# Both scan directions in one process: their small products alternate between the two column halves of the matrix array

## The chip, the cores and the metric

The kernel runs on one core of one Trainium2 chip. The metric is the device time of one execution in microseconds (us), lower is better. The core's engines work in parallel, each through its own instruction queue in order: TensorE (PE, matrix products, with its weight loads shown apart as PEld), VectorE (DVE), ScalarE (ACT), GpSimd (POOL), and SyncE (SP), which starts transfers. A product takes its operands from the 128 partitions of the on-chip memory and writes into the 128 partitions of the accumulator memory, which has banks of 512 columns.

## The reference

One encoder layer is applied to two request groups, a prompt of 512 tokens and a sample of 1024 tokens, of width 1024. It has a SwiGLU block, a mixer and a second SwiGLU block, each with normalisation, shift, scale and gate. Half of the mixer's channels go through windowed averages, the other half (8 heads of 64 channels) through a recurrence that runs over the tokens once forwards and once backwards:

```python
def step(S, inp):
    r_t, w_t, k_t, v_t, na_t, b_t = inp
    sa = jnp.einsum('bhvk,bhk->bhv', S, na_t)
    S = S * w_t[:, :, None, :] + sa[..., None] * b_t[:, :, None, :] + v_t[..., None] * k_t[:, :, None, :]
    y = jnp.einsum('bhvk,bhk->bhv', S, r_t)
    return S, y
...
ys.append(wkv_scan(r, decay, k_d, v, kk, a, reverse=(d == 1)))
...
y = ys[0] + ys[1]
```

## The kernel before

**Dense work.** Tokens are handled in three blocks of 512 (two of the sample, one of the prompt). The SwiGLU blocks, the mixer's input and its output projection are products of 128x128 weights with 128x512 activations. Each is done as three products of a split number: `whi`, `wlo` are the upper and lower parts of the weights, `hh`, `hl` (and `gh`, `gl`) those of the activations; `u`, `v` and `y` are the banks in which the results stand. One generator (`mainA`, then `mainB` and `mainC`) issues all dense work in a fixed sequence, and where it needs something that isn't there yet, it stops.

**The scan.** The recurrence is done in chunks of `L` = 64 tokens, for two heads at a time (one head on partitions 0 to 63, the other on 64 to 127). There are 8 pairs of heads and group, and they make 12 "macros" of 8 chunks: 96 chunks in each of the two directions `d`. `scan_prep` makes the operands of a macro half (4 chunks), `scan_inv` inverts its triangular matrices, `scan_state` carries the 64x64 states `SBD` through the chunks, and `scan_post` normalises the output. `MU` holds three operand arrays: `MA` and `MR` (64x64 matrices of a chunk) and `UV`. For every chunk and direction `scan_state` has three stages:

- W: the product of `AR` with the state (`sb<-SBD,AR` in the profile: 128 rows of the array, 64 columns, 128 moving elements; left out in the first chunk of a pair) and two 64x64 products of `MA` with `UV` (`sb<-MU`, 64*64), all into `Wp`; ScalarE copies `Wp` to `iw` (`XN<-sb`) and writes the state times the chunk's decay to `s0p`;
- U: two 64x64 products with `iw` (`sb<-XN,MU`) into `Up`; ScalarE copies them to `UV` (`MU<-sb`);
- the state's increment (`sb<-MU,BKt`, 128 rows) and the output (`sb<-AR,SBD`, 64 rows, and `sb<-MU` with 128 rows), where the two heads' products write to partitions 0 to 63 and 64 to 127 in turn; VectorE then makes the new state from the increment and `s0p`.

Each direction has a bank of its own (`sb` with the number 9080 for the forward one, 9081 for the backward one). In it `Wp` and `Up` stand on partitions 0 to 63 in both directions. A product of 32-bit numbers is two records in the trace, each with a weight load.

**What sets the order.** The program is planned while it is built. Every generator is a process; a `yield WAIT` gives back control, and `run_until` starts the process of the smallest `prio` number whose last result should be there by a table of estimated durations (`Estimate`). The two directions were two processes, `scan_state(sb, 0)` and `scan_state(sb, 1)`, both of `prio` 0, and the dense generator (`prio` 3) fills what is left, one product at a time. Each engine then executes its instructions in that order. While the scan is going on (`scanning`), the lower halves `wlo` of the weights are made by VectorE, otherwise by GpSimd or VectorE. All engine instructions carry line 161 in the profile, since one helper issues them; they are told apart by their tiles.

Of the kernel before, what the change touches and what calls it, by code (L numbers as in the profile page):

```python
# [12 lines left out]
AF = mybir.ActivationFunctionType  # L13
ALU = mybir.AluOpType
# [3 lines left out]
P = 128  # L18
# [5 lines left out]
L = 64  # L24
# [14 lines left out]
GO, WAIT, CHAIN, PIPE = -1.0, -2.0, -3.0, -4.0  # L39
# [133 lines left out]
def encoder_kernel(ctx, tc, x_prompt, x_sample, c_prompt, c_sample, ada_w, ada_b, n1_pre, n1_post,  # L173
# [5 lines left out]
    V, S, G, T, SY = (Queue(est, *q) for q in (("V", nc.vector), ("S", nc.scalar), ("G", nc.gpsimd), ("T", nc.tensor),  # L179
                                               ("Y", nc.sync)))  # L180
# [21 lines left out]
    def mt(shape, tag, bufs, dt=F32, pool=None):  # L202
        return est.ring((pool or mp).tile(shape, dt, name=nm(tag), tag=tag, bufs=bufs), (id(pool), tag), bufs)
# [10 lines left out]
    def spawn(gen, prio):  # L214
        procs.append(Proc(gen, prio))

    def run_until(stop):

        while not stop():
            clock = est.free["T"]
            for p_ in procs:
                if p_.cond is not None and p_.cond():
                    p_.cond = None
                    p_.ready = max(p_.ready, clock)
            live = [p_ for p_ in procs if p_.cond is None]
            assert live
            now = [p_ for p_ in live if p_.ready <= clock]
            if now:  # L230
                p_ = min(now, key=lambda q: q.prio)
            else:
                p_ = min(live, key=lambda q: q.ready)
                est.free["T"] = p_.ready
            est.last = 0.0
            try:
                r = next(p_.gen)
            except StopIteration:
                procs.remove(p_)
                continue  # L240
            if callable(r):
                p_.cond = r
            elif isinstance(r, tuple):
                p_.ready = r[0]
            elif r == GO:
                p_.ready = 0.0
            elif r == PIPE:
                p_.ready = est.last - PIPE_LEAD
            elif r == CHAIN:
                p_.ready = est.last - CHAIN_LEAD  # L250
            else:
# [700 lines left out]
    GT = (TB, 2 * TB)  # L952
# [192 lines left out]
    GL = 4 * L  # L1145

    def st_(sb, shape, tag, bufs=1):
        return mt(shape, tag, bufs, pool=sb.sp)
# [180 lines left out]
            flags.add(("inv", m, gi))  # L1329
            give("inv")  # L1330

    def scan_state(sb, d):
        AR, BKt, UV, MA, MR, SBD, PL, bank = sb.AR, sb.BKt, sb.UV, sb.MA, sb.MR, sb.SBD, sb.PL, sb.bank[d]
        Wp = bank[0:64, 0:P]
        Up = bank[0:64, P:2 * P]
        for m, (i_, hf) in enumerate(macros):
            g, p = pairs[i_]
            nblk = GT[g] // GL
            nh = nblk // 2
            for c8 in range(8):  # L1340
                gi, c = c8 // 4, c8 % 4
                if c == 0:
                    yield has(("inv", m, gi))
                zero = hf == 0 and c8 == 0
                lastc = hf == nh - 1 and c8 == 7
                us = [gi * 16 + d * 8 + h * 4 + c for h in range(2)]
# [12 lines left out]
                S.activation(UV[0:64, gi, d, c].rearrange("p h f -> p (h f)"), Up, AF.Copy)  # L1359
                yield WAIT  # L1360
                if not lastc:
                    for h in range(2):
                        hs_ = slice(64 * h, 64 * h + 64)
                        mm(bank[hs_, 0:L], BKt[:, gi, d, c, hs_], UV[:, gi, d, c, h, :])
                yo = 256 + c * L
                if not zero:
                    for h in range(2):
                        hs_ = slice(64 * h, 64 * h + 64)
                        mm(bank[hs_, yo:yo + L], SBD[hs_, d, hs_], AR[hs_, gi, d, c, 1, :], stop=False)
                for h in range(2):  # L1370
                    mm(bank[64 * h:64 * h + 64, yo:yo + L], UV[:, gi, d, c, h, :], MR[:, us[h], :], start=zero)
                if not lastc:
                    for h in range(2):
                        hs_ = slice(64 * h, 64 * h + 64)
                        pl_ = PL[hs_, m % 2, gi, d, c:c + 1]
                        if zero:
                            V.tensor_scalar(SBD[hs_, d, hs_], bank[hs_, 0:L], pl_, None, op0=ALU.mult)
                        else:
                            V.scalar_tensor_tensor(SBD[hs_, d, hs_], bank[hs_, 0:L], pl_, s0p[hs_, hs_],
                                                   ALU.mult, ALU.add)  # L1380
                if c == 3:
                    t = 2 * hf + gi
                    gb = t if d == 0 else nblk - 1 - t
                    if t == 0 and i_ not in sb.yT:
                        if i_ >= 1:
                            yield has(("post", i_ - 1))
                        if i_ not in sb.yT:
                            sb.yT[i_] = st_(sb, [P, GT[g]], "yT")
                    o = sb.yT[i_][:, gb * GL:(gb + 1) * GL]
                    if d == 1:  # L1390
                        o = rev(o)
                    if t >= nh:
                        V.tensor_tensor(o, o, bank[:, 256:512], ALU.add)
                    else:
                        S.activation(o, bank[:, 256:512], AF.Copy)
                    flags.add(("st", m, gi, d))
                yield WAIT

    def scan_post(sb):
# [181 lines left out]
    with tc.tile_pool(name="late", bufs=1, reuse_waits="tile") as lp:  # L1581
        sb = ScanBufs(lp)
        scanning.append(sb)

        spawn(scan_state(sb, 0), 0)
        spawn(scan_state(sb, 1), 0)
        spawn(scan_inv(sb, 0), PRIO_INV)
        spawn(scan_inv(sb, 1), PRIO_INV)
        spawn(scan_prep(sb), PRIO_PREP)
        spawn(scan_post(sb), PRIO_POST)  # L1590

        run_until(has(("m", 1), ("m", 0)))
        scanning.clear()
# [35 lines left out]
```

## Time and profile before

| | |
|---|---|
| median of 3 runs | 3785.25 us (3784.39 to 3792.8) |
| the profiled execution | 3780.28 us; its span from the first to the last instruction 3778.3 us |
| busy share of the span: PE, DVE, ACT, POOL | 95%, 53%, 38%, 37% |
| instructions of PE | 19579 products, as many weight loads |
| the scan | from 1270 us to 2698 us of the span |
| mean granted clock of PE | 0.956 |

Busy time counts an instruction from its start to its modelled end, and products are pipelined, so a busy PE can still be issued faster or slower: how many microseconds a group of products takes is read from the starts of its first product and of the next group's first. The granted clock is the share of PE's full clock over a stretch; a row of the timeline merges neighbours of one kind and gives their first start, and "xcount" is the number of records.

### The profile page before, as it was taken

Reading aid. Unit: us, or ns where it says so; the run is one execution under the profiler, and the core shown is the slowest. Engines: PE = TensorE matmul, PEld = TensorE weight load, DVE = VectorE, ACT = ScalarE, POOL = GpSimd, SP = SyncE. Lnnn points to the kernel's source line nnn. Section 1 sums busy time; section 2 is a strip of 40 time slices with the busy share of each in tenths; the row PEclk is TensorE's granted clock in tenths of the full one; section 3 lists DMA queues with packets and bytes.
Section 4 is the critical chain, followed back from the end, with each engine's and each line's share of the span. In section 5 each row is a group of like instructions: output and inputs, shape, how many; then the busy total and the mean of one; then the engine's idle time right before and its main releaser. Section 6 shows DMA issues by size and latency. Waiting matters only on the chain. (4 is left out here: it accounts for less than half of the span.)

```text
span 3778.3 us, 53665 instructions
## 1 busy us (share of the span) xinstructions
PE 3593.2 (95%) x19579; PEld 2703.6 (72%) x19579; DVE 1999.0 (53%) x3801; ACT 1424.1 (38%) x2776; POOL 1410.4 (37%) x1716
## 2 busy tenths in 40 slices
PE   7999999998999999999899989799999999999998
PEld 4667878876676767666666666567787778877886
DVE  3128362237237778776777776778448622242223
ACT  3324342225335434344345433343334432234222
POOL 2333444443132222234234233432344344444444
PEclk8999999998999999999889978599999999999999
DMA  7655343334344322222324343222254333334332
GB/s 274 235 181 169 91 154 92 99 90 134 123 128 126 93 67 88 82 71 87 117 76 122 96 137 105 74 73 77 87 159 151 103 115 98 93 109 132 94 95 78
DMA packets 557980, 432.11 MB, mean 114 GB/s; under 512 B 27029, under 2 KB 511572, under 8 KB 553620
## 3 DMA queue, kind: packets, MB, share of 16 engines
q1 hardware_dynamic: 524900, 379.90, 32.8%
q10 hardware_dynamic: 32816, 48.78, 4.1%
q8 instruction: 155, 2.54, 0.3%
q14 instruction: 109, 0.89, 0.1%
HBM read 367.23 MB, written 61.34 MB: 113 GB/s over the span
## 5 line engine op out<-in xcount | busy, mean ns | idle before, releaser
L161 POOL TENSOR_TENSOR wlo<-wraw,whi 128x512 fp32r<-128x512 f32 x672 | 892.6, 1346 | 1294.2 <-ACT whi L161 866.5
L161 DVE TENSOR_TENSOR y<-y,y 128x512 f32<-128x512 f32 x480 | 327.2, 684 | 848.9 <-PE y L161 847.9
L161 ACT ACTIVATE whi<-wraw 128x512 fp32r<-128x512 f32 x938 | 559.2, 622 | 181.6 <-PE v L161 139.7
L161 PE MATMUL u<-hh,whi 128*128 128x512 f32 x1392 | 568.2, 408 | 10.2 <-ACT zraw L161 4.0
L161 PE MATMUL u<-hl,whi 128*128 128x512 f32 x1392 | 564.3, 405 | 14.1 <-POOL hl L161 7.4
L161 PE MATMUL v<-hh,whi 128*128 128x512 f32 x1392 | 562.4, 404 | 12.8 <-ACT hh L161 7.6
L161 PE MATMUL u<-hh,wlo 128*128 128x512 f32 x1392 | 567.0, 407 | 0.1
L161 PE MATMUL v<-hl,whi 128*128 128x512 f32 x1392 | 561.0, 403 | 1.0 <-DVE hl L161 1.0
L161 PE MATMUL v<-hh,wlo 128*128 128x512 f32 x1392 | 560.7, 403 | 0.0
L161 PE MATMUL y<-gh,whi 128*128 128x512 f32 x1056 | 425.6, 403 | 12.8 <-DVE y L161 10.8
L161 PE MATMUL y<-gl,whi 128*128 128x512 f32 x1056 | 422.7, 400 | 0.2 <-DVE gl L161 0.2
L161 PE MATMUL y<-gh,wlo 128*128 128x512 f32 x1056 | 422.2, 400 | 0.0
L161 POOL TENSOR_TENSOR XN<-XN 64x126 f32<-64x126 f32 (+22 forms) x744 | 322.4, 433 | 93.6 <-DVE XN L161 18.5
L161 PEld LDWEIGHTS u<-hl,whi 128*128 128x128 f32 x1392 | 266.6, 191 | 81.5 <-DVE hl L161 12.6
L161 ACT ACTIVATE gh<-s 128x512 fp32r<-128x512 f32 x132 | 83.3, 631 | 639.3 <-DVE s L161 639.3
L161 PEld LDWEIGHTS u<-hh,whi 128*128 128x128 f32 x1392 | 266.3, 191 | 80.9 <-issue 7.7
L161 PEld LDWEIGHTS v<-hh,whi 128*128 128x128 f32 x1392 | 264.2, 190 | 82.9 <-ACT hh L161 11.3
L161 PEld LDWEIGHTS u<-hh,wlo 128*128 128x128 f32 x1392 | 266.3, 191 | 68.8 <-issue 9.5
L161 PEld LDWEIGHTS v<-hl,whi 128*128 128x128 f32 x1392 | 264.4, 190 | 66.3 <-issue 4.9
L161 PEld LDWEIGHTS v<-hh,wlo 128*128 128x128 f32 x1392 | 264.8, 190 | 62.9 <-issue 5.9
L161 DVE TENSOR_TENSOR wlo<-wraw,whi 128x512 fp32r<-128x512 f32 x266 | 206.4, 781 | 150.6 <-ACT whi L161 149.8
L161 PEld LDWEIGHTS y<-gh,whi 128*128 128x128 f32 x1056 | 199.9, 189 | 67.2 <-DVE y L161 12.0
(252 smaller groups left out, 4504.6 us busy)
## 6 DMA issues: line engine op xcount, KB each, us to landing
wraw<-in_f_w_dram SPq DMA_DIRECT2D x792, 256.0 KB
ada<-in_ada_w_dram SPq DMA_DIRECT2D x32, 1024.0 KB
wraw<-in_w_in_dram SPq DMA_DIRECT2D x98, 256.0 KB
xk<-xs ACTq DMA_DIRECT2D x96, 256.0 KB
xs<-y ACTq DMA_DIRECT2D x48, 256.0 KB
wraw<-in_w_out_dram SPq DMA_DIRECT2D x48, 256.0 KB
in_k<-zk SPq DMA_DIRECT2D x48, 128.0 KB
in_kk<-zkk SPq DMA_DIRECT2D x48, 128.0 KB
```

What stands on the lines that cost most here:

```text
L161: return f(*args, **kw)
```

## The change

There is now one process for both directions. W of both directions is issued together, then U of both, then the third stage of both. In W and U the products alternate between the directions, and the backward direction's `Wp` and `Up` stand on partitions 64 to 127 of its bank, so that neighbouring products use different halves of the array's columns. The four copies by ScalarE stand together in pairs, and the two `s0p` come behind the copies of `Up` and no longer behind the first copy of `Wp`. In the third stage the increments of both directions come first and then, per direction, the output products. Number, shape and operands of the scan's products are the same.

```diff
-    def scan_state(sb, d):
+    def scan_state(sb):
...
+        half = [slice(64 * h, 64 * h + 64) for h in both]
+        Wp = [sb.bank[d][half[d], 0:P] for d in both]
+        Up = [sb.bank[d][half[d], P:2 * P] for d in both]
...
                 if not zero:
-                    mm(Wp, AR[:, gi, d, c, 0, :], SBD[:, d, :], stop=False)
-                for h in range(2):
-                    mm(Wp[:, h * L:(h + 1) * L], MA[64:128, us[h], :], UV[64:128, gi, d, c, h, :], start=zero)
-                wsb = sb.iw[:, d * P:(d + 1) * P]
-                S.activation(wsb, Wp, AF.Copy)
+                    for d in both:
+                        mm(Wp[d], AR[:, gi, d, c, 0, :], SBD[:, d, :], stop=False)
+                for h in both:
+                    for d in both:
+                        mm(Wp[d][:, hl_(h)], MA[64:128, us(d, h), :], UV[64:128, gi, d, c, h, :], start=zero)
+                for d in both:
+                    S.activation(wsb[d], Wp[d], AF.Copy)
+                yield WAIT
+                for h in both:
+                    for d in both:
+                        mm(Up[d][:, hl_(h)], MA[0:64, us(d, h), :], wsb[d][:, hl_(h)])
+                for d in both:
+                    S.activation(UV[0:64, gi, d, c].rearrange("p h f -> p (h f)"), Up[d], AF.Copy)
                 if not zero and not lastc:
-                    s0p = st_(sb, [P, P], f"s0p{d}")
-                    S.activation(s0p, SBD[:, d, :], AF.Copy, scale=PL[:, m % 2, gi, d, c:c + 1])
-                yield WAIT
-                for h in range(2):
-                    mm(Up[:, h * L:(h + 1) * L], MA[0:64, us[h], :], wsb[:, h * L:(h + 1) * L])
-                S.activation(UV[0:64, gi, d, c].rearrange("p h f -> p (h f)"), Up, AF.Copy)
+                    for d in both:
+                        s0p[d] = st_(sb, [P, P], f"s0p{d}")
+                        S.activation(s0p[d], SBD[:, d, :], AF.Copy, scale=PL[:, m % 2, gi, d, c:c + 1])
                 yield WAIT
                 if not lastc:
-                    for h in range(2):
...
+                    for d in both:
+                        for h in both:
+                            mm(sb.bank[d][half[h], 0:L], BKt[:, gi, d, c, half[h]], UV[:, gi, d, c, h, :])
...
-        spawn(scan_state(sb, 0), 0)
-        spawn(scan_state(sb, 1), 0)
+        spawn(scan_state(sb), 0)
```

PE's queue before, at the second chunk of the scan: W of the forward direction (`sb_9080`), W of the backward one (`sb_9081`), three dense products, and the forward U.

```order
L161 MATMUL sb_9080<-SBD_9077,AR_9073 64x128
L161 MATMUL sb_9080<-MU_9075 64x64 x2
L161 MATMUL sb_9081<-SBD_9077,AR_9073 64x128
L161 MATMUL sb_9081<-MU_9075 64x64 x2
L161 MATMUL v_10093<-hh_8728,whi_9961 128x512
L161 MATMUL v_10093<-hl_8729,whi_9961 128x512
L161 MATMUL v_10093<-hh_8728,wlo_9962 128x512
L161 MATMUL sb_9080<-XN_9076,MU_9075 64x64 x2
```

The same W now:

```order
L161 MATMUL sb_9080<-SBD_9077,AR_9073 64x128
L161 MATMUL sb_9081<-SBD_9077,AR_9073 64x128
L161 MATMUL sb_9080<-MU_9075 64x64
L161 MATMUL sb_9081<-MU_9075 64x64
L161 MATMUL sb_9080<-MU_9075 64x64
L161 MATMUL sb_9081<-MU_9075 64x64
L161 MATMUL v_10081<-hh_8728,wlo_9962 128x512
```

The four groups of W have become two, each of them alternating between the directions.

PE's queue before, at U of the same chunk (the product in front of the first row is dense, and the next U is the next chunk's):

```order
L161 MATMUL sb_9080<-XN_9076,MU_9075 64x64 x2
L161 MATMUL v_10093<-hh_8728,whi_9961 128x512
L161 MATMUL v_10093<-hl_8729,whi_9961 128x512
L161 MATMUL sb_9081<-XN_9076,MU_9075 64x64 x2
L161 MATMUL v_10093<-hh_8728,wlo_9962 128x512
```

And now:

```order
L161 MATMUL v_10081<-hh_8728,wlo_9962 128x512
L161 MATMUL sb_9080<-XN_9076,MU_9075 64x64
L161 MATMUL sb_9081<-XN_9076,MU_9075 64x64
L161 MATMUL sb_9080<-XN_9076,MU_9075 64x64
L161 MATMUL sb_9081<-XN_9076,MU_9075 64x64
L161 MATMUL v_10081<-hh_8728,whi_9961 128x512
```

Dense products stood between the two directions' U, and now they stand in front of and behind both. In the whole program such a pair of U was divided in 78 of 96 chunks, and is now in none; the stretches of other work between two dense products of the scan's time are 379 and were 483.

ACT's queue before, in the next chunk (`s0p` is the decayed state, `XN<-sb` the copy of W, `MU<-sb` that of U):

```order
L161 ACTIVATE XN_9076<-sb_9080 64x128
L161 ACTIVATE s0p_10142<-SBD_9077,PL_9079 128x128
L161 ACTIVATE XN_9076<-sb_9081 64x128
L161 ACTIVATE s0p_10148<-SBD_9077,PL_9079 128x128
L161 ACTIVATE whi_10152<-wraw_9916 128x512
L161 ACTIVATE MU_9075<-sb_9080 64x128
L161 ACTIVATE MU_9075<-sb_9081 64x128
```

And now:

```order
L161 ACTIVATE XN_9076<-sb_9080 64x128
L161 ACTIVATE XN_9076<-sb_9081 64x128
L161 ACTIVATE MU_9075<-sb_9080 64x128
L161 ACTIVATE MU_9075<-sb_9081 64x128
L161 ACTIVATE s0p_10108<-SBD_9077,PL_9079 128x128
L161 ACTIVATE s0p_10110<-SBD_9077,PL_9079 128x128
L161 ACTIVATE whi_10124<-wraw_9916 128x512
```

The two `s0p` have moved from between the copies to behind them.

The plan of everything else moves with it, since the same planner sets it. At one place the dense generator has stopped (it waits for the block's normalisation after the prompt's first SwiGLU). PE's queue there before, with the directions at different stages and preparation products (`sM`) among them:

```order
L161 MATMUL sb_9080<-XN_9076,MU_9075 64x64 x2
L161 MATMUL sb_9081<-SBD_9077,AR_9073 64x128
L161 MATMUL sb_9081<-MU_9075 64x64 x2
L161 MATMUL sb_9080<-MU_9075,BKt_9074 64x64 x2
L161 MATMUL sb_9080<-AR_9073,SBD_9077 64x64 x2
L161 MATMUL sb_9080<-MU_9075 64x64 x2
L161 MATMUL sM_15818<-in_wa_15717,w2s_151 128x256
L161 MATMUL sM_15819<-in_wa_15717,w2s_151 128x256
L161 MATMUL sb_9081<-XN_9076,MU_9075 64x64 x2
```

And PE's queue there now, where U follows W, and the increment follows U, with nothing between:

```order
L161 MATMUL sb_9080<-MU_9075 64x64
L161 MATMUL sb_9081<-MU_9075 64x64
L161 MATMUL sb_9080<-XN_9076,MU_9075 64x64
L161 MATMUL sb_9081<-XN_9076,MU_9075 64x64
L161 MATMUL sb_9080<-XN_9076,MU_9075 64x64
L161 MATMUL sb_9081<-XN_9076,MU_9075 64x64
L161 MATMUL sb_9080<-MU_9075,BKt_9074 64x64 x2
L161 MATMUL sb_9081<-MU_9075,BKt_9074 64x64 x2
```

One direction's stage stood between the other's, and now both directions stand at the same stage. Over all, 7210 of the program's 11556 dense products were issued by the end of the scan, and now 7265 are.

More of the change, by code (lines that the diff above doesn't have):

```diff
@@ L1330, in scan_inv @@
             give("inv")
-    def scan_state(sb, d):
-        AR, BKt, UV, MA, MR, SBD, PL, bank = sb.AR, sb.BKt, sb.UV, sb.MA, sb.MR, sb.SBD, sb.PL, sb.bank[d]
-        Wp = bank[0:64, 0:P]
-        Up = bank[0:64, P:2 * P]
+    def scan_state(sb):
+        AR, BKt, UV, MA, MR, SBD, PL = sb.AR, sb.BKt, sb.UV, sb.MA, sb.MR, sb.SBD, sb.PL
+        both = range(2)
+        half = [slice(64 * h, 64 * h + 64) for h in both]
+        Wp = [sb.bank[d][half[d], 0:P] for d in both]
+        Up = [sb.bank[d][half[d], P:2 * P] for d in both]
+        hl_ = lambda h: slice(h * L, (h + 1) * L)
         for m, (i_, hf) in enumerate(macros):
@@ L1345, in scan_state @@
                 lastc = hf == nh - 1 and c8 == 7
-                us = [gi * 16 + d * 8 + h * 4 + c for h in range(2)]
+                us = lambda d, h: gi * 16 + d * 8 + h * 4 + c
+                wsb = [sb.iw[:, d * P:(d + 1) * P] for d in both]
+                s0p = {}
                 if not zero:
-                    mm(Wp, AR[:, gi, d, c, 0, :], SBD[:, d, :], stop=False)
-                for h in range(2):
-                    mm(Wp[:, h * L:(h + 1) * L], MA[64:128, us[h], :], UV[64:128, gi, d, c, h, :], start=zero)
@@ L1360, in scan_state @@
+                if not zero and not lastc:
+                    for d in both:
+                        s0p[d] = st_(sb, [P, P], f"s0p{d}")
+                        S.activation(s0p[d], SBD[:, d, :], AF.Copy, scale=PL[:, m % 2, gi, d, c:c + 1])
                 yield WAIT
                 if not lastc:
-                    for h in range(2):
-                        hs_ = slice(64 * h, 64 * h + 64)
-                        mm(bank[hs_, 0:L], BKt[:, gi, d, c, hs_], UV[:, gi, d, c, h, :])
-                yo = 256 + c * L
@@ L1366, in scan_state @@
[L1366 to L1371, printed above, removed]
-                if not lastc:
[L1373 to L1380, printed above, removed]
+                    for d in both:
+                        for h in both:
+                            mm(sb.bank[d][half[h], 0:L], BKt[:, gi, d, c, half[h]], UV[:, gi, d, c, h, :])
@@ new lines, in scan_state @@
+                yo = slice(256 + c * L, 256 + c * L + L)
+                for d in both:
+                    if not zero:
+                        for h in both:
+                            mm(sb.bank[d][half[h], yo], SBD[half[h], d, half[h]], AR[half[h], gi, d, c, 1, :], stop=False)
+                    for h in both:
+                        mm(sb.bank[d][half[h], yo], UV[:, gi, d, c, h, :], MR[:, us(d, h), :], start=zero)
+                if not lastc:
+                    for d in both:
+                        for h in both:
+                            pl_ = PL[half[h], m % 2, gi, d, c:c + 1]
+                            if zero:
+                                V.tensor_scalar(SBD[half[h], d, half[h]], sb.bank[d][half[h], 0:L], pl_, None, op0=ALU.mult)
+                            else:
+                                V.scalar_tensor_tensor(SBD[half[h], d, half[h]], sb.bank[d][half[h], 0:L], pl_,
+                                                       s0p[d][half[h], half[h]], ALU.mult, ALU.add)
@@ L1381, in scan_state @@
                 if c == 3:
                     t = 2 * hf + gi
-                    gb = t if d == 0 else nblk - 1 - t
-                    if t == 0 and i_ not in sb.yT:
+                    if t == 0:
                         if i_ >= 1:
                             yield has(("post", i_ - 1))
[L1387 to L1396, printed above, removed]
+                        sb.yT[i_] = st_(sb, [P, GT[g]], "yT")
+                    for d in both:
+                        gb = t if d == 0 else nblk - 1 - t
+                        o = sb.yT[i_][:, gb * GL:(gb + 1) * GL]
+                        if d == 1:
+                            o = rev(o)
+                        if t >= nh:
+                            V.tensor_tensor(o, o, sb.bank[d][:, 256:512], ALU.add)
+                        else:
+                            S.activation(o, sb.bank[d][:, 256:512], AF.Copy)
+                        flags.add(("st", m, gi, d))
```

## The prediction

> **What bounds the kernel now.** I read the page's busy shares first, then the windows of the scan and of its tile `sb`, then PE's waits there, then PE's timeline.
>
> ```profile
> PE 3593.2 (95%) x19579; PEld 2703.6 (72%) x19579; DVE 1999.0 (53%) x3801; ACT 1424.1 (38%) x2776; POOL 1410.4 (37%) x1716
> 1270.00:2698.00 1428.00, 1344.32 (x9601) 948.84 (x9599) 1035.48 (x2319) 590.55 (x1358) 478.18 (x923) 0.91 0.29 89
> 1270.00:2698.00 1428.00, 389.91 (x4064) 268.08 (x4064) 108.75 (x376) 107.66 (x408) 0.91 0.29 89
> PE sM L161 <- DVE MU L161: 24.4, 20, 5.4
> PE sb L161 <- DVE SBD L161: 10.1, 11, 2.1
> PE sb L161 <- ACT MU L161: 5.1, 5, 3.2
> PE sb L161 <- ACT XN L161: 4.2, 5, 1.9
> ```
>
> PE is busy for 95% of the span. In the scan's 1428 us (third row, columns: length, then busy time of PE, PEld, DVE, ACT, POOL, then clock and DMA) it is busy for 1344 us and DVE for 1035 us (73%). The scan's own products are seen for 390 us (fourth row). The waits of PE on the scan's copies and states are 10.1 + 5.1 + 4.2 us in all, so the scan's chain is mostly covered by other products, and what a scan product costs is the time in which PE can't issue the next one. That is read from starts in the timeline (start, modelled length, group), at full clock:
>
> ```profile
> 1500.55 0.68 PE L161 MATMUL sb<-XN,MU 64*64 64x64 f32 x8
> 1501.15 0.50 PE L161 MATMUL u<-hl,whi 128*128 128x512 f32 x1
> ...
> 1502.68 0.34 PE L161 MATMUL sb<-MU,BKt 128*64 128x64 f32 x4
> 1502.84 0.29 PE L161 MATMUL sb<-MU 128*64 128x64 f32 x4
> 1502.96 0.29 PE L161 MATMUL sb<-MU,BKt 128*64 128x64 f32 x4
> 1503.08 0.29 PE L161 MATMUL sb<-MU 128*64 128x64 f32 x4
> 1503.29 0.50 PE L161 MATMUL u<-hl,whi 128*128 128x512 f32 x1
> ...
> 1503.97 0.43 PE L161 MATMUL sb<-SBD,AR 128*64 128x128 f32 x2
> 1504.33 0.44 PE L161 MATMUL sb<-MU 64*64 64x64 f32 x4
> 1504.70 0.43 PE L161 MATMUL sb<-SBD,AR 128*64 128x128 f32 x2
> 1505.07 0.44 PE L161 MATMUL sb<-MU 64*64 64x64 f32 x4
> 1505.44 0.50 PE L161 MATMUL y<-gh,whi 128*128 128x512 f32 x1
> ...
> 1506.33 0.44 PE L161 MATMUL sb<-XN,MU 64*64 64x64 f32 x4
> 1506.70 0.51 PE L161 MATMUL y<-gh,whi 128*128 128x512 f32 x1
> ...
> 1508.18 0.34 PE L161 MATMUL sb<-MU,BKt 128*64 128x64 f32 x4
> 1508.44 0.33 PE L161 MATMUL sb<-AR,SBD 64*64 64x64 f32 x4
> 1508.70 0.34 PE L161 MATMUL sb<-MU 128*64 128x64 f32 x4
> 1508.97 0.50 PE L161 MATMUL v<-hh,whi 128*128 128x512 f32 x1
> 1509.31 0.40 PE L161 MATMUL v<-hl,whi 128*128 128x512 f32 x1
> 1509.54 0.39 PE L161 MATMUL v<-hh,wlo 128*128 128x512 f32 x1
> 1509.86 0.43 PE L161 MATMUL sb<-SBD,AR 128*64 128x128 f32 x2
> ```
>
> Two prices are to be seen. Four records of U, all on the lower half of the columns, take 0.37 us (1506.33 to 1506.70) and eight take 0.60 us (1500.55 to 1501.15): 0.058 us for each further record. The increment and output products already alternate between the column halves, as their two heads write to different halves: four take 0.26 to 0.27 us (1508.18 to 1508.97), and sixteen of one kind take 0.61 us (1502.68 to 1503.29), which is 0.029 us for each further record, half as much. So eight alternating records should cost 0.265 + 4 x 0.029 = 0.38 us.
>
> **The change part by part.**
>
> W, in the 88 chunks with a state (96 chunks less the first of 8 pairs): before, 1.47 us for both directions (1503.97 to 1505.44). Now two groups. Four `sb<-SBD,AR` records, alternating: the trace has none, so the bounds are those of two records, 0.36 us (1503.97 to 1504.33), if they run side by side, and 0.58 us, if two more of 0.11 us (twice the 0.058 us, for 128 elements instead of 64) stand behind them. I take 0.37, by the nearest row, the alternating increments of the same 128x64 weights. The eight `sb<-MU` records take 0.38. That is 0.75 us, and 0.72 us saved: 88 x 0.72 = 63 us. In the 8 first chunks there are only the eight `sb<-MU` records, which stood together before (0.60): 8 x 0.22 = 2 us.
>
> U: 78 chunks had two groups of 0.37, 18 had one of 0.60; now it is one of 0.38 in all: 78 x 0.36 + 18 x 0.22 = 32 us.
>
> Dense neighbours: a plain dense product takes 0.23 us (1509.31 to 1509.54), the first after a small group 0.34 (1508.97 to 1509.31), the last before one 0.32 (1509.54 to 1509.86). Each stretch of small work among the dense thus costs 0.2 us, and the order has 379 of these for 483: 104 x 0.2 = 21 us.
>
> Third stage: before, 0.79 us per direction (1508.18 to 1508.97). Where both stood together, the backward increments ran on from the forward output at 0.16 (1502.84 less 1502.68) instead of 0.265, so 1.48 for both; now 0.38 + 4 x 0.26 = 1.43. By the order about 51 pairs stood together and 37 apart: 51 x 0.05 + 37 x 0.15 = 8 us.
>
> Copies and states: the same instructions on ACT and DVE. The new costs are hand-overs, at which both directions now wait. The scan's waits by operation:
>
> ```profile
> 1504.81 0.27 ACT L161 ACTIVATE XN<-sb 64x128 f32<-64x128 f32 x1 [0.30 <-PE sb L161]
> 1504.98 0.39 ACT L161 ACTIVATE s0p<-SBD,PL 128x128 f32<-128x128 f32 x1
> 1505.55 0.27 ACT L161 ACTIVATE XN<-sb 64x128 f32<-64x128 f32 x1 [0.17 <-PE sb L161]
> 1509.17 0.58 DVE L161 SCALAR_TENSOR_TENSOR SBD<-sb,PL,s0p 64x64 f32<-64x64 f32 x2 [2.19 <-PE sb L161]
> ```
>
> The group of 1505.07 ends at 1505.51 and its copy begins at 1505.55; an instruction on ACT follows another after 0.17 us, so both copies are done 0.04 + 0.17 + 0.27 = 0.48 us after W's end. PE could go on 0.07 us before W's end (1505.44), so it waits 0.55 us if nothing stands between, and two or three dense products cover it. By the order, W to U has four dense products in half of the chunks and none in 16, U to the increment eight in half and none in 9. From the increment to the next W there are four state updates on DVE (2 x 0.58, about 1.1 us) under four output groups (1.04 us). Price: 25 x 0.55 us and some 0.3 us in 8 chunks without dense work, 16 us. What is queued behind a waiting U or W on PE is dense work, which then comes later; who waits for that are DVE's sums `y`, off the path.
>
> `s0p` leaves the path from W to U on ACT (0.39 us) and now stands ahead of the state update, under the increment: nothing. 17 additions and subtractions of 128x512 move from POOL to DVE by the order, under PE's time. 55 dense products come before the scan's end instead of behind it: no change of their number. The remaining waits of PE on DVE's bursts (24.4 us on `MU`) grow as PE gets faster: I take 10 us, between 0 and once more the 43.8 us of the four rows above.
>
> Sum: 63 + 2 + 32 + 21 + 8 = 126 us of PE time, less 16, less 10: 100 us. All of it is priced at full clock. The profiled execution took 3780.28 us (span 3778.3), 5 us under the median of 3785.25; the forecast against the median is 3685 us.
>
> One rule speaks against the price. Row first: the alternating records on 128 rows take 0.029 us each. The Trainium skill, "TensorE: Matmul & The Clock Gate", Part 3 (The mechanism), has weight loads overlap running products only when the row group differs; new W and U neighbours share their rows and differ in columns. By that rule nothing would overlap, and the sum is that of the first rival. The rows of the increment, which share all 128 rows, disagree with it.
>
> **The rivals.**
>
> (1) *The neighbours don't run side by side.* For: no row of before has 64-row products on the same rows and different column halves. Against: the increments of 128 rows do it. Then W is 0.58 + 0.60 for 1.47 (0.29 x 88 = 25 us), U 78 x 0.14 = 11 us, neighbours 21 and third stage 8 as before: 65 us, less 26: 39 us, 3746 us.
>
> (2) *DVE or the copies come late.* PE loses 9% of the scan's time, DVE's 1035 us stay, 80% of what is left. For: PE already waits 24.4 us for `MU`. If half of the 126 us turns into waits, 3722 us.
>
> (3) *The clock.* The scan has stretches with no dense products, in which the granted clock is lower:
>
> ```profile
> 1850.00:1920.00 70.00, 58.69 (x371) 40.80 (x369) 49.73 (x90) 32.23 (x70) 40.20 (x71) 0.59 0.32 95
> 2362.00:2445.00 83.00, 63.85 (x380) 44.99 (x381) 60.77 (x122) 33.69 (x71) 43.69 (x73) 0.53 0.19 62
> 1906.01 0.69 PE L161 MATMUL sb<-XN,MU 64*64 64x64 f32 x4
> 1906.63 0.79 PE L161 MATMUL u<-hh,whi 128*128 128x512 f32 x1
> ```
>
> There U takes 0.62 us instead of 0.37. The mean clock of the scan is 0.91. At 0.95 the scan would be some 4% shorter (57 us, where PE bounds): 3628 us; at 0.87 as much longer: 3742 us. For the worse: the order has six chunks nearly without dense work at the place of the first row, where there were three. For the better: small groups among dense ones get shorter, and the same products take less of these stretches.
>
> (4) *Slower: the directions in step.* Each chunk has three hand-overs at which no other direction's stage fills in, 288 in all. If each left PE 0.44 us without work (126 / 288), nothing would be gained, and from 0.47 us on the kernel would be slower by over 0.2% (7.6 us, about what a measurement of this kernel can tell). Uncovered they cost 0.55 us: 288 x 0.55 = 158 us, so 3817 us. Against it: the order covers all but some 33 of them.
>
> **How the numbers follow.** The forecast (side by side, most of the sum arrives, 3640 to 3720) gets 0.60; rival 1 0.07, rival 2 0.13, rival 3 0.07 for the better and 0.07 for the worse, rival 4 0.06. From 3630 to 3750 lie the forecast, rivals 1 and 2, and half of 3: 0.87, taken as 0.8, for the sizes are uncertain. The forecast alone reaches from 3640 to 3720. Slower by over 0.2%: rival 4, 0.06; within 0.2%: the ends of rivals 2 and 3, 0.04; faster: 0.90.
>
> **What the profile of the changed kernel would show.** Right: a group of eight `sb<-XN,MU` records takes 0.38 us to the next dense start, W 0.75 us; the scan from its first to its last `sb` shrinks by some 85 to 90 us net of the 55 dense products (13 us) that it takes in, and what lies behind it by 13 us. Rival 1: eight records take 0.60. Rival 2: waits of PE for DVE well above 50 us in the scan. Rival 3: the scan's mean clock outside 0.89 to 0.93. Rival 4: waits of PE `sb` on ACT and DVE of 100 us or more. I would be wrong if the waits that the trace shows as covered are covered by just the products that get shorter.

## The result, and the profile after

The changed kernel takes 3761.52 us (median of 4 runs, 3759.12 to 3768.02), the kernel before beside it 3784.82 us. The ratio is 0.9939 (95%: 0.9924 to 0.9954): 23 us faster, where 100 had been forecast. The profiled execution took 3768.02 us, its span is 3764.7 us.

The rows of after that answer to those of before: PE's line of the page, the windows of the scan (all instructions, then the tile `sb`), and PE's waits there, in us in total, times and longest.

```profile
PE 3528.1 (94%) x19579; PEld 2669.6 (71%) x19579; DVE 2008.0 (53%) x3818; ACT 1436.5 (38%) x2774; POOL 1394.5 (37%) x1699
1270.00:2698.00 1428.00, 1293.48 (x9677) 927.44 (x9677) 1050.92 (x2347) 608.90 (x1369) 468.61 (x911) 0.86 0.30 90
1270.00:2698.00 1428.00, 303.21 (x4064) 208.20 (x4064) 108.79 (x376) 114.01 (x408) 0.86 0.30 90
PE sM L161 <- DVE MU L161: 30.6, 21, 5.5
PE sb L161 <- DVE SBD L161: 25.0, 24, 4.4
PE sb L161 <- ACT XN L161: 16.8, 8, 6.3
PE sb L161 <- ACT MU L161: 10.2, 7, 4.9
```

PE's busy time in the scan fell by 51 us (1344.3 to 1293.5), that of the scan's own products by 87 us (389.9 to 303.2). The scan still takes as long: from its first to its last `sb` product 1427.0 us before and 1422.5 after. Two columns took the saving. PE's idle time in that stretch went from 83.5 to 134.0 us, and the granted clock from 0.91 to 0.86.

The prices of the products are those forecast. PE's timeline of after, at full clock, first at a U, then at a W (start, modelled length, group):

```profile
1282.10 0.45 PE L161 MATMUL sb<-XN,MU 64*64 64x64 f32 x8
1282.48 0.50 PE L161 MATMUL v<-hh,whi 128*128 128x512 f32 x1
...
1287.07 0.44 PE L161 MATMUL sb<-SBD,AR 128*64 128x128 f32 x4
1287.44 0.45 PE L161 MATMUL sb<-MU 64*64 64x64 f32 x8
1287.82 0.50 PE L161 MATMUL v<-hh,whi 128*128 128x512 f32 x1
```

U takes 0.38 us (1282.10 to 1282.48), W 0.37 + 0.38 = 0.75 us, as in the prediction. To see what became of it, the scan's stretch is accounted for in one way for every kernel below. "PE work" is PE's busy time there less half of the busy time under half clock (what it would be at full clock), less 0.23 us for each 128x512 product, as their number changes. "Clock" is that half.

| profiled execution | PE work | dense in the scan | idle | clock | scan's length |
|---|---|---|---|---|---|
| before | 618 | 2666 | 83.5 | 112 | 1427.0 |
| after | 505 | 2723 | 134.0 | 157 | 1422.5 |

PE work fell by 113 us (126 forecast). Of these, 50.5 went to idle time, 45 to a lower clock, and 13 to the 57 dense products more; 4.5 us are left in the scan, and behind the scan the span is 12 us shorter. The two profiled executions lie 12 us apart (3780.28 and 3768.02) and the medians 23, so this account is of a pair in which the change gained less than usual; after's profiled execution is the slowest of its four, with the lowest clock (0.938; the others 0.939 to 0.941).

**Where the lead is lost.** The dense generator's sequence is the same in both kernels, so its progress can be compared product by product:

| us of the span | before | after |
|---|---|---|
| last product of the prompt's first SwiGLU | 1819.4 | 1769.1 |
| last product of the mixer's second input part | 2170.3 | 2133.9 |
| last windowed average ahead of block 0's output projection | 2229.6 | 2213.6 |
| first product of block 0's output projection | 2264.7 | 2265.3 |
| last dense product | 3761.0 | 3747.4 |

After is 50 us ahead at 1769 us, 16 us at 2214 us, and behind by 0.6 us at the output projection. So 34 us of the lead are lost between the first SwiGLU and the last windowed average, and 17 in the stop ahead of the output projection. The account by stretch (before / after, in us):

| stretch of the scan | length | idle | clock |
|---|---|---|---|
| up to the last product of the prompt's first SwiGLU | 549 / 496 | 19 / 22 | 13 / 17 |
| from there to the last windowed average | 410 / 445 | 30 / 53 | 44 / 76 |
| the stop ahead of the output projection | 35 / 52 | 7 / 14 | 10 / 17 |
| from there to the scan's end | 433 / 431 | 28 / 45 | 44 / 47 |

In the second stretch, with the same dense products in both and one chunk of the scan more in after, PE idles for 22 us more and loses 32 us more to the clock. The scan itself comes no earlier: U of its 33rd, 64th and 96th (last) chunk starts at 1731.1, 2231.1 and 2694.8 us before, and at 1737.4, 2226.0 and 2693.7 after.

The output projection reads the scan's normalised output of the block, which needs the scan's 64th chunk. Behind this chunk's U the normalisation runs through PE, DVE and POOL and two transfers: to the projection's first product it takes 33.5 us before and 39.4 after. While the generator stops, PE has little but the scan. PE's timeline of before around the stop, and the windows row of the stop (in a timeline row, the brackets hold idle time and what ended it):

```profile
2229.59 0.40 PE L161 MATMUL u<-hh,wlo 128*128 128x512 f32 x1
...
2231.13 0.27 PE L161 MATMUL sb<-XN,MU 64*64 64x64 f32 x1
...
2264.67 0.80 PE L161 MATMUL u<-hh,whi 128*128 128x512 f32 x1
2229.00:2265.00 36.00, 29.31 (x252) 22.28 (x248) 24.87 (x66) 12.21 (x30) 11.21 (x24) 0.67 0.43 143
```

The row at 2231.13 is the start of the 64th chunk's U. The same of after, where that U is the row at 2225.97:

```profile
2213.59 0.40 PE L161 MATMUL u<-hh,wlo 128*128 128x512 f32 x1
...
2216.79 0.78 PE L161 MATMUL sb<-MU,BKt 128*64 128x64 f32 x8 [0.26 <-ACT MU L161]
...
2223.63 1.32 PE L161 MATMUL sb<-SBD,AR 128*64 128x128 f32 x4 [4.41 <-DVE SBD L161]
2224.88 0.69 PE L161 MATMUL sb<-MU 64*64 64x64 f32 x8
2225.97 0.98 PE L161 MATMUL sb<-XN,MU 64*64 64x64 f32 x8 [0.40 <-ACT XN L161]
...
2237.85 1.88 PE L161 MATMUL sM<-MU 32*32 32x32 f32 x32 [2.10 <-DVE MU L161]
...
2265.34 0.80 PE L161 MATMUL u<-hh,whi 128*128 128x512 f32 x1 [1.17 <-ACT hh L161]
2213.00:2265.00 52.00, 38.53 (x305) 27.64 (x303) 35.59 (x98) 14.12 (x37) 15.88 (x32) 0.57 0.34 109
```

The stop grew from 35 to 52 us: PE comes there sooner and waits for the same chunk and its normalisation. In these 52 us PE is idle for 13.5 us at a mean clock of 0.57, and cheaper products shorten it little, since most of the chain goes through other engines. One link of it, on DVE of after, ahead of the state update (the 64th chunk's) for which PE waits 4.41 us:

```profile
2218.27 0.41 DVE L161 SCALAR_TENSOR_TENSOR cs<-ta,sg 128x256 f32<-128x256 f32 x1
2218.61 0.41 DVE L161 TENSOR_TENSOR cs<-in_wa,sg 128x256 f32<-128x256 f32 x1
2218.94 0.47 DVE L161 SCALAR_TENSOR_TENSOR ta<-in_wa,vB,in_r 128x256 f32<-128x256 f32 x1
2220.25 0.48 DVE L161 SCALAR_TENSOR_TENSOR ta<-in_wa,vB,in_r 128x256 f32<-128x256 f32 x1 [0.84 <-POOL bq L161]
2220.65 2.31 DVE L161 TENSOR_TENSOR XN<-XN 64x135 f32<-64x135 f32 x6
2222.99 1.21 DVE L161 SCALAR_TENSOR_TENSOR SBD<-sb,PL,s0p 64x64 f32<-64x64 f32 x4
```

The increment ended at 2217.57 us (2216.79 + 0.78), and the update `SBD` began at 2222.99: for 5.4 us it stood in DVE's queue behind the preparation of a later macro half (`cs`, `ta`, and the inversion's `XN<-XN`).

### The profile page after: what moved, and what is told of

It reads as the page before. It is cut to its first block, busy times and chain, and to the rows that moved or that the text cites. A ratio compares the mean times of both kernels' runs of the same rounds, so it can differ in the third digit from the quotient of the medians.

```text
span 3764.7 us, 53675 instructions
## 1 busy us (share of the span) xinstructions
PE 3528.1 (94%) x19579; PEld 2669.6 (71%) x19579; DVE 2008.0 (53%) x3818; ACT 1436.5 (38%) x2774; POOL 1394.5 (37%) x1699
## 5 line engine op out<-in xcount | busy, mean ns | idle before, releaser
L161 PE MATMUL v<-hh,whi 128*128 128x512 f32 x1392 | 566.2, 407 | 13.5 <-ACT hh L161 5.6
L161 ACT ACTIVATE gh<-s 128x512 fp32r<-128x512 f32 x132 | 83.5, 632 | 638.0 <-DVE s L161 637.6
```

Source lines behind the costliest of these rows:

```text
L161: return f(*args, **kw)
```

## The experiments

Each ran beside the kernel before on the same chip (its medians there: 3784.5 to 3786.2 us). Whole kernels first, then cut ones, then whole ones again.

**The layout alone, and the merging alone.** On the kernel before, in its order:

```diff
-        Wp = bank[0:64, 0:P]
-        Up = bank[0:64, P:2 * P]
+        Wp = bank[64 * d:64 * d + 64, 0:P]
+        Up = bank[64 * d:64 * d + 64, P:2 * P]
```

> Two processes as before and the same order of instructions; only the backward direction's W and U stand on partitions 64 to 127. Theory A (the gain comes from neighbours on different column halves, so both parts of the change are needed): the directions' products meet only at seams (88 pairs of W, 18 of U), so within 8 us of before, 3777 to 3790 us, clock of the scan 0.91. Theory B (the layout alone makes the products cheaper): 3740 to 3765 us.

3790.21 us, ratio 1.0013 (1.0003 to 1.0023): nothing gained, at the upper edge of theory A's range. Theory B (the layout alone) is out. The other half of the change, on the changed kernel, with its order of products:

```diff
-        Wp = [sb.bank[d][half[d], 0:P] for d in both]
-        Up = [sb.bank[d][half[d], P:2 * P] for d in both]
+        Wp = [sb.bank[d][half[0], 0:P] for d in both]
+        Up = [sb.bank[d][half[0], P:2 * P] for d in both]
```

> One process and exactly the order of the changed kernel, but W and U of both directions on partitions 0 to 63, so the neighbours share the column half. W and U take some 0.65 us more of PE per chunk at full clock (0.60 for 0.38 twice, and 0.58 for 0.37), about 61 us. Theory A (PE's granted clock follows how many columns PE streams, and the cheaper products let it fall in stretches with little dense work): the scan's mean clock rises from 0.86 to about 0.90, and 30 us or more of the 61 come back: 3765 to 3800 us. Theory B (the directions in step make PE wait, and the waits lower the clock): clock stays 0.85 to 0.87 and the time is 3820 us or more.

3777.54 us, 0.9976 (0.9961 to 0.999). Its timeline at the same places:

```profile
1278.54 0.67 PE L161 MATMUL sb<-XN,MU 64*64 64x64 f32 x8
1279.15 0.50 PE L161 MATMUL v<-hh,whi 128*128 128x512 f32 x1
...
1283.74 0.65 PE L161 MATMUL sb<-SBD,AR 128*64 128x128 f32 x4
1284.32 0.67 PE L161 MATMUL sb<-MU 64*64 64x64 f32 x8
1284.93 0.50 PE L161 MATMUL v<-hh,whi 128*128 128x512 f32 x1
```

In the same order, U takes 0.61 us for 0.38 and W 0.58 + 0.61 for 0.37 + 0.38. So running side by side is real, and saves 57 us of PE work (562 to 505), of which only 16 us are in the time. The time lies in theory A's range (3765 to 3800), and the scan's clock is 0.89 for 0.86: of the 57 us, after has 34 more of clock loss and 19 more of idle time than this kernel in the profiled executions. These two lie at the fast end of the one kernel's runs (3769.71, median 3777.54) and the slow end of the other's, so a part of the 34 us is the scatter from run to run.

**More work for PE where it idles.** On the changed kernel, a process of the lowest priority issues a useless product (128x64 weights, 128 moving elements) wherever the planner has nothing else (423 products), to hold the clock up:

```diff
+    def fill_gen(sb):
+        out = sb.bank[1][0:64, P:2 * P]
+        while scanning:
+            mm(out, ident[:, 0:64], ident)
+            yield GO
...
+        spawn(fill_gen(sb), 9)
```

> The changed kernel with 423 added products (128x64 weights, 128 moving elements, into an unused corner of a scan bank, results not used), issued by a process of the lowest rank wherever the planner would leave PE idle during the scan. At full clock they are about 0.22 us each, 93 us of PE. Theory A (low clock in the sparse stretches is what ate the gain): the scan's clock rises from 0.86 to over 0.92 and the time falls, 3725 to 3755 us. Theory B (the scan's chain of copies and states ate it, the clock only follows): the products stand in the chain's way, 3775 to 3840 us.

3801.48 us, 1.0042 (1.0027 to 1.0057). The clock rose, in the scan to 0.92:

```profile
1270.00:2730.00 1460.00, 1340.91 (x10467) 988.26 (x10467) 1048.39 (x2340) 604.20 (x1360) 470.72 (x909) 0.92 0.29 88
```

It gave back 51 us (clock 157 to 106), and the fillers added 107 us of PE work (505 to 612). The time lies in theory B's range (3775 to 3840), and theory A's 3725 to 3755 is missed. PE's waits of `sb` for `XN`, ACT's `MU` and `SBD` rose to 70.2 us from 52.0. So the clock can be held up, but not with these products, which cost more than they give back. It says little on the cause.

**A larger delay between chunks.** `AFTER_STATE`, the time that the planner leaves after a result before it takes the state process up again, on the changed kernel:

```diff
-AFTER_STATE = 200
+AFTER_STATE = 500
```

> The changed kernel with the planner's delay behind a scan stage raised from 200 to 500 ns, so that more dense products stand between the stages of a chunk. PE's waits for the scan's copies and states are 52 us in the changed kernel. Theory B (hand-overs of the directions in step): these waits halve, and the time falls by 15 to 35 us, to 3725 to 3747 us. Theory A (the sparse stretches have no dense products to put there): the waits fall by under 15 us and the time stays within 10 us of the changed kernel, 3752 to 3772 us.

3785.28 us (3762.86 to 3799.6 in 10 runs), 1.0003 (0.9987 to 1.002). Neither expected time held. The waits for copies and states fell by 7 us (52.0 to 44.9), as theory A had it, but the profiled execution, the fastest of the ten, has more idle time (141 us) and a scan of the same length. From run to run the time moved by 37 us with the mean clock (0.943 in the fastest, 0.929 in the slowest). Why the clock is lower here no run shows.

**Without the output projection's wait.** In both kernels, block 0's output projection reads the windowed averages' half in place of the scan's half, which its product leaves out; then it needn't wait for the 64th chunk:

```diff
-        spawn(mload_gen([(("m", 0, "h"), 0, 4, 0, ("m", 1))]), PRIO_NORM)
+        spawn(mload_gen([(("m", 0, "h"), 0, 0, 0, ("z", 1))]), PRIO_NORM)
```

> The kernel before, but the first block's output projection takes the pooled half of the mixer's output where it should take the scan's half, so it doesn't wait for the scan's first 64 chunks (of the result, that part is left out). Theory C (the dense work gets ahead and then stops until the scan's 64th chunk is through, at 2265 us in both kernels, and so the gain up to there is lost): the 35 us between the last dense product of the stage in front and the first of the projection are partly filled, 3745 to 3780 us. Theory A (the low clock alone ate the gain): 3770 to 3790 us.

> The changed kernel with the same part left out. In it the gap is 52 us. Theory C: what was gained up to there is kept, and it is 40 to 60 us under the kernel before with the same cut (changed against before uncut: 23 us). Theory A: 15 to 30 us under it, as uncut.

Before: 3789.0 us, 1.001 (0.9998 to 1.0021). After: 3738.11 us, 0.9878 (0.9857 to 0.9898). The kernel before gains nothing from it, in theory A's range and outside theory C's (29 of the 36 us of its stop held work that PE has to do anyway, which may be why); the changed one gains 23 us. The change itself is now worth 51 us for 23, as theory C had it (40 to 60). How much of that the missing wait brings is taken up with the three pairs below. PE's timeline of the cut changed kernel at the same place:

```profile
2198.73 0.39 PE L161 MATMUL u<-hh,wlo 128*128 128x512 f32 x1
...
2204.64 0.50 PE L161 MATMUL u<-hh,whi 128*128 128x512 f32 x1 [1.02 <-ACT hh L161]
```

The stop shrank to 5.9 us, and the generator is 45 us ahead of the cut kernel before (2204.6 for 2249.7 us).

**A shorter preparation.** 15 of the 31 steps of the triangular inversion are left out, in both kernels; they run on POOL and DVE, and PE's products stay the same in number:

```diff
-            for j in range(31, 0, -1):
+            for j in range(31, 15, -1):
```

> The kernel before with 16 of the 31 steps of the scan's triangular inversion on VectorE and GpSimd (the rest is left out). By the order the scan's 64th chunk then comes 570 dense products earlier. Theory C: the scan's pace is set by preparation and inversion, not by the products of the change; the projection no longer waits for it: 3690 to 3750 us. Theory A: the inversion is hidden, within 20 us of before, 3765 to 3805 us.

> The changed kernel with the same cut. Theory C: with the wait for the scan gone the cheaper products come through, 50 to 110 us under the kernel before with the same cut. Theory A (sparse stretches with a low clock): not more than 35 us under it.

Before: 3808.83 us, 1.0057 (1.0042 to 1.0072); after: 3726.51 us, 0.9841 (0.9826 to 0.9856). A faster chain costs the kernel before 23 us, against the expectation (the cut lets the scan come ahead of the dense work: 2331 dense products in its stretch for 2666, with a lower clock; I didn't follow it further). The same cut gains the changed kernel 35 us. The change is worth 82 us with it, in theory C's range of 50 to 110; 23 of these are what the kernel before loses by the cut.

**Side by side, without the wait.** The cut of the output projection's wait on the merging alone:

> The changed kernel's order, W and U of both directions on the same column half, and the projection that doesn't wait (the same part left out). Only the place of the backward W and U differs from the changed kernel with that cut (3738 us). With the wait the same difference was 16 us (3777.5 against 3761.5), of 61 us of PE time. Theory C (the wait for the scan hid the rest): 30 to 60 us over it, 3768 to 3798 us. Theory B (the copies and states of directions in step bound the chunks): under 25 us, 3745 to 3763 us.

3762.51 us, 0.9943 (0.9928 to 0.9958). Merging is worth 26 us here (3789.0 to 3762.5; 8 with the wait), side by side 24 (16 with it). Theory C's 30 us or more for side by side were not there; theory B's range (3745 to 3763) held.

**Both cuts.** What was still open is whether waits on the scan's pace explain the whole shortfall.

> Before, with both cuts: the output projection of block 0 reads the windowed half in place of the scan's half (which is left out there), and 15 of 16 of the 31 inversion steps... that is all but the first 16, are left out. Both theories: neither cut alone made the kernel before faster (3789 and 3809 us), so 3785 to 3815 us.

> The same order of products as both_after, with W and U of both directions on one column half, and the same two cuts. Theory C: side by side is now worth 45 to 61 us, so both_after is that much faster than this. Theory D: 20 to 35 us, as with one cut (24 us).

> The changed kernel with the same two cuts. Theory C (the gain is lost where PE waits for the scan's pace: at block 0's output projection and at the macro boundaries): without both, the forecast's 100 us arrive, 90 to 110 us below both_before. Theory D (the cheaper products keep PE less busy, so the granted clock falls, and that takes back a part wherever the waits are): the difference stays at 50 to 85 us, with a mean clock lower than that of both_before by 0.005 or more.

Before 3809.1 us, 1.0059 (1.0043 to 1.0076); merging alone 3753.38, 0.9914 (0.9898 to 0.9929); after 3725.49, 0.9835 (0.982 to 0.985). The difference is 84 us: theory C's 90 to 110 is missed, and so is theory D's sign, as the clocks are equal (0.946 and 0.947). The second cut adds nothing to the first (3726.5 to 3725.5): with a faster preparation the output projection no longer has to wait, so both cuts remove the same stop. Side by side is worth 28 us here: theory C's 45 to 61 is missed, theory D's 20 to 35 held. Windows of the scan's stretch, both cuts, before and after:

```profile
1252.00:2622.00 1370.00, 1276.46 (x9267) 909.91 (x9265) 923.18 (x1951) 576.32 (x1327) 327.79 (x561) 0.88 0.28 87
```

```profile
1251.00:2566.00 1315.00, 1206.71 (x9395) 866.08 (x9391) 932.17 (x1966) 603.71 (x1349) 335.60 (x564) 0.88 0.30 93
```

DVE's and POOL's columns show what was cut (1035 to 923 us, 478 to 328), PE's clock is 0.88 in both. The cut makes the preparation shorter and takes load off DVE and POOL at once; the runs don't separate the two. Now the account of the three pairs, unchanged against changed; all columns but the last are of the profiled executions:

| pair | PE work saved | new idle time | new clock loss | time gained | time gained (medians) |
|---|---|---|---|---|---|
| whole | 113 | 50.5 | 45 | 12 | 23 |
| without the wait | 98 | 43.5 | 1 | 57 | 51 |
| without the wait, short preparation | 89 | 15 | -10 | 86 | 84 |

The PE work saved is similar in each (some less where fewer pairs of U were divided: 66 in the last, 78 in the first). What it brings depends on whether the scan's pace lets PE use it: with the short preparation the new idle time falls from 50.5 to 15 us, and U of the last chunk comes 55 us earlier (2618.5 to 2563.2) where it came 1 us earlier in the whole pair.

The clock column of the first two rows can't be put down to the stop. Up to the stop, PE's order of instructions is the same in a kernel and in its cut without the wait, so the cut changes nothing there. Yet from the scan's start to that place the clock took 57.6 us in before and 75.9 in its cut, 94.2 in after and 72.8 in its cut. That makes 40 of the 44 us by which the two rows differ, from one execution (or chip) to another. In time, 29 of the 45 us between 12 and 57 had arisen when the last windowed average was issued (before 2229.6, its cut 2243.8, after 2213.6, its cut 2198.7); 16 arose at the stop and behind it, about the 17 us of lead that the stop took in the whole pair. How the 28 us of the medians (23 to 51) divide no run shows.

**Making the chunks come earlier.** Three delays of the planner, on the changed kernel and on the one before: after a result the state process is taken up at once, other processes too, and a chain's process up to 0.6 us ahead of its estimated result.

```diff
-AFTER_STATE = 200
-AFTER_OTHER = 400
-CHAIN_LEAD = 300
+AFTER_STATE = 0
+AFTER_OTHER = 0
+CHAIN_LEAD = 600
```

> The changed kernel, whole, with the planner's three delays changed (AFTER_STATE 200 to 0, AFTER_OTHER 400 to 0, CHAIN_LEAD 300 to 600), so that the scan's 64th chunk comes 98 dense products (some 23 us) earlier in the order. Theory C: the projection starts at 2235 to 2250 us instead of 2265 and the time is 3725 to 3750 us. Theory B (chunks in step bound by their hand-overs): more waits of PE on the scan's copies and states, 3755 us or more.

> The kernel before with the three delays of the first of these. Its 64th chunk comes 245 dense products earlier in the order. Theory C: its products leave PE no time, so the earlier scan brings little: its gap of 35 us ahead of the projection goes, but PE waits elsewhere; 3765 to 3795 us. If the delays alone are good for any version, it falls by as much as the changed kernel, 3750 us or less.

> The same with CHAIN_LEAD left at 300: the 64th chunk comes 65 dense products earlier. Theory C: 3730 to 3755 us. Theory B: 3755 us or more.

> The changed kernel, whole, with CHAIN_LEAD 600 for 300 alone (a chain's process may be taken up 0.6 us ahead of its estimated result). Theory C: the scan's chunks come earlier, so most of the 10 us that the three delays together gave: 3748 to 3758 us. Rival: it needs the other two delays as well, and it stays at 3758 to 3775 us.

All three on the changed kernel: 3751.4 us (3749.25 to 3754.08), 0.9912 (0.9897 to 0.9927), the best whole version here, 10 us under the changed kernel and between the two theories' ranges; the projection starts at 2257.3 us, later than theory C's 2235 to 2250. On the kernel before the same three cost 63 us, which no theory had: 3848.78, 1.0173 (1.0148 to 1.0197). The first two alone on the changed kernel lose 12 us, against theory C: 3773.91, 0.9968 (0.9955 to 0.998). The third alone: 3757.57, 0.9924 (0.9901 to 0.9947), at the edge of theory C's range and, by its four runs (3750.35 to 3768.88), not told apart from its rival. In the best version the first SwiGLU of the prompt ends later than in the changed kernel (1831.9 for 1769.1 us), and the stop ahead of the output projection is 9.7 us (2247.6 to 2257.3) for 51.7: what stood in front of the wait was given to the scan. In the kernel before the scan then takes in 188 dense products fewer, and the clock takes 177 us in it for 112; my reading is that the dense work has no lead to give there. These delays, and the one of 500 ns above, move the changed kernel between 3751 and 3785 us, so differences of 10 to 20 us between two planned orders can come from the plan as a whole and not from the thing that was varied.

## Why the prediction was wrong

By its own steps:

- **Prices: right.** U 0.38 and W 0.75 us to the hundredth, and rival 1's prices (0.58, 0.60) were those of the merging alone to 0.01 us. PE work fell by 113 us for 126. The Trainium skill, "TensorE: Matmul & The Clock Gate", Part 3 (The mechanism), has loads overlap only with other row groups; here products on the same rows and different column halves overlap (eight take 0.38 us for 0.61), and the measurement decides. The Trainium skill, "TensorEngine Tiling (Array Packing)", Key Properties, says that different tiles load and multiply in parallel; that agrees.
- **The step that failed** is the reading of the 20 us of PE waits: "the scan's chain is mostly covered by other products, and what a scan product costs is the time in which PE can't issue the next one". With both directions in step these waits rose to 52 us, and the idle time by 50.5 (31 of them in the merging alone, 19 by side by side). The scan's chunks kept their pace (the last U at 2694.8 us before, 2693.7 after), and the saved PE work became idle time and, in the profiled executions, lost clock. One place where this shows is a stop of the dense generator: the next dense product is released by the scan's pace, and PE work saved ahead of that point only makes PE come sooner to the same wait. No term of the sum and no rival had the stop at 2265 us, though before shows a 35 us hole in the dense products there; it takes 17 us of a lead of 50, and 34 are lost ahead of it. With a shorter preparation the new idle time is 15 us for 50.5, and the change is worth 82 to 84 us.
- **Less 16 for hand-overs, less 10 for DVE's bursts** was 26; the idle time grew by 50.5 us. PE's waits of `sb` for `XN`, ACT's `MU` and `SBD` rose from 19.4 to 52.0 us, 33 for the 16 priced; that is the term that was mis-sized. Those of `sM` for `MU` rose only from 24.4 to 30.6, within the 10. The merging alone brings nearly all of these waits (15.3, 9.5 and 24.4 us), so they don't come of the shorter products; that no other direction's stage is there to fill in fits with it.
- **Priced at full clock.** The scan's mean clock fell from 0.91 to 0.86, outside of the 0.89 to 0.93 named, for 45 us in the profiled executions. Rival 3 had the size for 0.87 (57 us) and a place (more chunks without dense work). How far the clock is a cause of its own stays open: over the runs after's mean clock is lower (0.938 to 0.941, before 0.950 to 0.957), but the same order of instructions lost 94 us to the clock in one execution and 73 in another, and with the short preparation the change doesn't lower the clock.
- **Rival 2** named waits for DVE above 50 us as its mark; `SBD` and `MU` alone are 55.6 us, and half of the saving did become idle time. It is nearest to what happened, yet its cause was DVE's load, while DVE has 73% of the scan before and 74% after. The state update shown above stood for 5.4 us behind other work in DVE's queue; how much such places make in all wasn't added up.
- **Rival 4** needed 100 us of `sb` waits; 52 came. Its mechanism, the directions in step, was there, at half of the size that it needed.
- The scan was to shrink "by some 85 to 90 us net of the 55 dense products (13 us) that it takes in, and what lies behind it by 13 us": the scan shrank by 4.5, the rest by 12.

The time lies 11.5 us above the range. What stays open: with both cuts 5 us of 89 are still missing, and of side by side's own saving (49 to 57 us of PE work in the three pairs) only 16, 24 and 28 us arrive, with 19 to 25 us of new idle time each. I didn't separate which hand-over takes that. Open, too, is how much of the whole pair's shortfall is the clock's, and why the kernel before loses 23 us by the shorter preparation.

## What to carry to other kernels

Before a saving on the busiest engine is booked as time, go through its work in order and look for places where it stops for something whose pace the saving doesn't touch; a saving ahead of such a place is worth only what the hole can't swallow. The share of waits in the trace of before is too small a sign, for a wait that is just covered costs nothing until the order around it changes. Where such a stop is found, it is worth trying to make the chain that releases it earlier: delays whose change cost the kernel before 63 us gained 10 in the changed one, though two of them alone lost 12. And before the difference of two traces is put down to an edit, compare them up to the first instruction that the edit changes: what differs there isn't the edit's doing.

## What the runs showed of the hardware

**The clock falls after a window in which few products were streamed.** The clock records of both kernels have two levels only, full and half, and change at a grid of 3.413 us. I counted for each such window the moving columns of PE's products. In before, all 19 windows after which the clock went down (the first 60 us and the kernel's end left out) had at most about 3400 columns (after: 28 windows, at most about 3500), the median window that kept full clock about 7400. A dense product of 512 columns takes 0.23 us, so 3400 columns are about 6.6 dense products in 3.413 us, not an idle PE: by the profile PE was busy for up to 71% of such a window in before. The Trainium skill, "TensorE: Matmul & The Clock Gate", Part 1, has two states and windows of this length; the trace agrees, and PE can lose its clock while busy. It is a bound and not a threshold: some windows with as few columns kept full clock, in before between 11 and 63 of 984 by the way of counting. Whether two products side by side count once or twice no run tested.

**From run to run the time follows the clock.** Over 25 runs of the kernel before, the time falls by 2.6 us for each 0.001 of mean clock (correlation -0.84), over 10 of the merging alone by 2.9 (-0.96), so a difference of a few us between two kernels is told apart by medians only. One execution can lose more than another with the same order of PE's instructions: 57.6 and 75.9 us of clock from the scan's start to 2231 and 2245 us in before and its cut, 94.2 and 72.8 to 2219 and 2203 us in after and its cut.
